# A ScalarE copy of one PSUM bank, and another buffer for one late weight, in a two-layer encoder trunk

## The chip, the cores and the metric

The kernel runs on one core of a Trainium2 chip. The metric is the device time of one execution in microseconds (us), as the median of several runs. Five engines work side by side, each through its own queue in order: PE (TensorE, matmuls), DVE (VectorE), ACT (ScalarE), POOL (GpSimd) and SP (SyncE). SP and POOL issue most of the transfers (DMA). A line number such as L1157 is a line of the kernel before; the changed kernel's lines lie 2 to 5 further down.

## The reference

One batch of 512 tokens with 1024 channels goes through two layers. Each layer has an input projection, four attention and convolution branches, a gated merge and an output projection, and then a feed-forward block:

```python
def _conv_ffn(h, w_up, conv_w, conv_b, w_down):
    u = _depthwise_conv(h @ w_up, conv_w, conv_b)
    gate, up = jnp.split(u, 2, axis=-1)
    return (jax.nn.silu(gate) * up) @ w_down

x = x + _conv_ffn(_rmsnorm(x, g_ffn[l]), w_up[l], ffn_conv_w[l], ffn_conv_b[l], w_down[l])
```

`w_up` is 1024 x 5632 (2816 gate and 2816 up channels), the depthwise convolution has width 3, all in float32. The change lies in `h @ w_up` of both layers.

## The kernel before

**Weights.** Every weight arrives as a tile of 128 x 1024 (`raw`, by a DMA of SP). ACT rounds it to `w_hi` (1.06 us), DVE subtracts to get `w_lo` (1.22 us), and PE sums three products, high by high, high by low and low by high. `w_hi` and `w_lo` have three buffers each, and weights are made two ahead of their use. `weights` (L239 and on) does this for plain weights, `seven_unit` (L1308 and on) for those below. The tiles of a plain weight come in turn from two buffers, tag `w_raw`; in the down projection, which comes next, two of four tiles come from two more, tag `w_more`.

**The up-projection.** It is cut into 11 groups of 2 x 256 output channels (two blocks of 128 gate channels and two of up channels). Groups 0, 1, 9 and 10 go as plain blocks. Groups 2 to 8 go as a product of 2 x 2 blocks with seven multiplications in place of eight: the units A11, S3, A22, S2, A12, S1, S4. A unit is 24 matmuls of 256 columns, a plain block 24 of 512. Three of the units' weights are loaded. The other four are sums of quarters and are made in the loaded tile: POOL adds a further quarter to it by an accumulating DMA (L1306) once the step before has made its `w_lo`. So A11, S3, S2 and S4 share one tile, called `chain` (tag `w_more`, two buffers, held from A11 to S4), and A22 and S1 share another (tag `w_raw`). When S4 of a group has made its `w_lo`, the chain buffer is free, and SP loads A11 of two groups on.

The groups are interleaved. Around group g, PE runs S2(g), A12(g), S1(g), S3(g+1), S4(g), A22(g+1), A11(g+2), then S2(g+1) and so on. At the end, where no further group follows, two plain blocks of group 9 are put among the last units, the `held` steps: ... A22(8), block 18.0, S2(8), A12(8), S1(8), block 18.1, S4(8). Their results stay in PSUM until they are taken out after S4(8).

**The banks.** A11, S2, S1 and S4 of a group add up in one PSUM bank (`aux`), and what it holds is taken out after each of them before the next may write. After A11, S3 and S2 it is ACT that copies the bank to an SBUF tile `sv` (L1145), ahead of other work (`with self.first()` raises the priority). After S1, DVE subtracts the bank from `sv` directly (L1157), also with raised priority. Then U0 is written (L1158), and `conv_part(…, 0)` computes the convolution of the gate blocks for both blocks of the group: an activation into cy0 on ACT (L1174), two updates on DVE (L1175, L1176), a silu on ACT (L1180). After S4 come U1 (L1162), cy1 in the same way, and the product f (L1191).

**The order.** The program's text gives the instructions, and a scheduler with priorities arranges each engine's queue when the kernel is built. Weight loading has raised priority over 3000 places. Within an engine the queue then runs in that order, each instruction waiting for its inputs and buffers.

Of the kernel before, what the change touches and what calls it, by code (L numbers as in the profile page):

```python
# [14 lines left out]
F32 = mybir.dt.float32  # L15
F32R = mybir.dt.float32r
I32 = mybir.dt.int32
AF = mybir.ActivationFunctionType
ALU = mybir.AluOpType
# [3 lines left out]
P = 128  # L23
L = 2
D = 1024
S = 512
KT = D // P
NB = S // P
DFF = 2816
# [9 lines left out]
def up_steps():  # L39

    whole = lambda g: [('whole', 2 * g + i, s) for i in range(2) for s in range(2)]
    slots = {}
    for i, g in enumerate(SEVEN):
        for n, at in (('A11', 0), ('S3', 4), ('A22', 6), ('S2', 8), ('A12', 9), ('S1', 10), ('S4', 12)):
            slots[7 * i + at] = ('seven', g, n)
    steps = [w for g in range(SEVEN[0]) for w in whole(g)]
    after = [w for g in range(SEVEN[-1] + 1, NP2) for w in whole(g)]
    own = [slots[t] for t in sorted(slots)]
    late = [('held',) + w[1:] for w in after[:2]]
    own = own[:-4] + late[:1] + own[-4:-1] + late[1:] + own[-1:]  # L50
    return steps[:-2] + own[:1] + steps[-2:] + own[1:] + [('free',) + w[1:] for w in after[:2]] + after[2:]


UP_STEPS = up_steps()

GATE_STEPS = [('ga', 'A11'), ('ga', 'A12'), ('gb', 'A11'), ('gb', 'A12'), ('ga', 'S3'), ('gb', 'S3'), ('ga', 'A22'),
              ('gb', 'A22'), ('ga', 'S2'), ('gb', 'S2'), ('ga', 'S1'), ('gb', 'S1'), ('ga', 'S4'), ('gb', 'S4')]
# [173 lines left out]
class Trunk:  # L231
# [7 lines left out]
    def weights(self, upto, ahead=3000, parts=1, queue=None):  # L239

        nc = self.nc
        while self.w_emitted < min(upto, len(self.w_list)):
            n, pieces = self.w_list[self.w_emitted]
            if n == 'seven':
                with self.tc.high_priority(offset=ahead):
                    self.w_ready.append(self.seven_unit(*pieces))
                self.w_emitted += 1
                continue
            with self.tc.high_priority(offset=ahead):

                self.w_fast = (self.w_fast + 1) % 4 if n == 0 else 0
                if n == 0 and self.w_fast in (3, 0):
                    raw = self.fp.tile([P, 1024], F32, name="w_raw", tag="w_more", bufs=2)
                else:
                    raw = self.wpool.tile([P, 1024], F32, name="w_raw", tag="w_raw", bufs=2)
                hi = self.wpool.tile([P, 1024], F32R, name="w_hi", tag="w_hi", bufs=3)
                lo = self.wpool.tile([P, 1024], F32R, name="w_lo", tag="w_lo", bufs=3)
                src = pieces()
                n = sum(p.shape[1] for p in src)
                if len(src) == 1:  # L260
                    cut = [slice(i * n // parts, (i + 1) * n // parts) for i in range(parts)]
                    src = [src[0][:, s] for s in cut]
                c = 0
                for p in src:
                    (queue or nc.sync).dma_start(raw[:, c:c + p.shape[1]], p)
                    c += p.shape[1]
                for i in range(parts):
                    s = slice(i * n // parts, (i + 1) * n // parts)
                    w = nc.scalar.activation(hi[:, s], raw[:, s], AF.Copy)  # L269
                    self.first_hi = self.first_hi or w  # L270
                    nc.vector.tensor_tensor(lo[:, s], raw[:, s], hi[:, s].bitcast(F32), ALU.subtract)  # L271
            self.w_ready.append((hi, lo))
            self.w_emitted += 1
# [842 lines left out]
    def seven(self, g, n):  # L1116

        nc = self.nc
        v = nc.vector
        st = self.sevens.setdefault(g, {})  # L1120
        bank = {'S3': 'B', 'A22': 'B', 'A12': 'C'}.get(n, 'A')
        start = n in ('S3', 'A11', 'A12')
        if start:
            st[bank] = self.mm() if bank == 'C' else self.aux()
        ps = st[bank]
        hi, lo = self.unit()
        for e in range(2):
            o = ps[:, e * 256:(e + 1) * 256]
            for j in range(4):
                s = slice((2 * j + e) * P, (2 * j + e + 1) * P)  # L1130
                xh, xl = self.seven_x(n, j)
                for i, (w, x) in enumerate(((hi, xh), (hi, xl), (lo, xh))):
                    self.last_mm = nc.tensor.matmul(o, lhsT=w[:, s], rhs=x, start=start and not (e or j or i),  # L1133
                                                    stop=j == 3 and i == 2, skip_group_check=True)
            if e == 0:
                self.tick()
        self.tick()
        two = lambda t: t.rearrange("p (e q) -> p e q", e=2)
        half = lambda h: self.RB[:, h * 256:(h + 1) * 256].unsqueeze(1).broadcast_to([P, 2, 256])
        place = lambda r, h: self.U[1 - r][:, :, 1 + h * 256:257 + h * 256]  # L1140
        tags = {'A11': 0, 'S3': 2, 'S2': 4}
        if n in tags:
            st[n] = self.fp.tile([P, S], F32, name="sv", tag=f"e{tags[n] + g % 2}", bufs=1)
            with self.first():
                nc.scalar.activation(st[n], ps, AF.Copy)  # L1145
        if n == 'S2':
            t = st['S2']
            v.tensor_tensor(t, st['B'], t, ALU.subtract)
            v.tensor_tensor(place(1, 0), two(t), half(0), ALU.mult)
        elif n == 'A12':  # L1150
            t = st['A11']
            v.tensor_tensor(t, t, ps, ALU.add)
            v.tensor_tensor(place(0, 0), two(t), half(0), ALU.mult)
        elif n == 'S1':
            t = st['S3']
            with self.first():
                v.tensor_tensor(t, t, ps, ALU.subtract)  # L1157
            v.tensor_tensor(place(1, 1), two(t), half(1), ALU.mult)  # L1158
            for i in range(2):
                self.conv_part(2 * g + i, 0)  # L1160
        elif n == 'S4':
            v.tensor_tensor(place(0, 1), two(ps), half(1), ALU.mult)  # L1162
            for i in range(2):
                self.conv_part(2 * g + i, 1)
# [70 lines left out]
    def ffn(self, l, last):  # L1235
# [12 lines left out]
        self.pace = 0.0  # L1248
        for kind, a, b in UP_STEPS:
            if kind == 'seven':  # L1250
# [267 lines left out]
    def run(self):  # L1518
        nc, tc = self.nc, self.tc
        with ExitStack() as st:  # L1520
# [10 lines left out]
            for l in range(L):  # L1531
                off, quads, quarters, ups, mixing = 0, [], {}, {}, []
                for kind, a, n in UNITS:
                    src = self.W[l, off:off + n * P].rearrange("(p c) -> p c", p=P)
                    off += n * P
                    if kind == 'quad':
                        quads.append(src)
                    elif kind == 'quarter':
                        quarters[a] = src
                    elif kind == 'up':  # L1540
                        ups[a] = src
                    elif kind == 'mixing':
                        mixing.append(src)
                    else:
                        if kind == 'out' and a == 0:
                            for i, (g, s) in enumerate(GATE_STEPS):
                                self.w_list.append(('seven', (l, g, s)))
                                if i >= 12:
                                    self.w_list.append((n, lambda m=mixing[i > 12]: [m]))
                        self.w_list.append((n, lambda src=src: [src]))  # L1550
                for kind, a, b in UP_STEPS:
                    if kind == 'seven':
                        self.w_list.append((kind, (l, a, b)))
                    elif kind != 'free':
                        self.w_list.append((1024, lambda src=ups[b * DFF + a * P]: [src]))
                self.quarters.append(quarters)
                self.quads.append(quads)
                self.sums.append([])
                self.all_quads.append(self.W[l, off - NP2 * 2048 * P:off].rearrange("(p c) -> p c", c=2048))
                self.last_units(l)  # L1560
# [10 lines left out]
            with tc.tile_pool(name="first", bufs=1, reuse_waits="tile") as first:  # L1571
# [4 lines left out]
                ps = self.aux()  # L1576
# [162 lines left out]
```

## Time and profile before

| | |
|---|---|
| median of the runs | 1534.66 us (1534.36 to 1537.81, 3 runs) |
| profiled execution | 1535.51 us, of which the profile's span is 1533.7 us |
| granted TensorE clock | 1.0 of full speed |
| up-projection, groups 2 to 8, layer 0 | about 463 to 627 us of the span |
| the same, layer 1 | about 1226 to 1391 us |
| ACT, making `w_hi` (L269, L1324) | 242.2, 75.9 and 56.9 us in its three groups |
| DVE, making `w_lo` (L271, L1325) | 280.5, 87.7 and 65.8 us in its three groups |
| load of a `w_raw` tile by SP, issue to landing | 4.4 us median |
| load or growth of a `chain` tile by POOL | 5.8 us median |

A row of the time view gives the start within the span, the duration, the engine, the line, the operation and its tiles; in brackets stands how long the engine sat idle before it and what ended that. A row of waits gives who waited for whom, the total, how often, and the longest. In a group of instructions, "x14 | 9.5, 680" means 14 instructions, 9.5 us busy together, 680 ns each on average. PE's matmuls are pipelined, so that each starts before the end drawn for the one ahead. Idle time of an engine matters only where PE, or what ends last, waits for it.

### The profile page before, as it was taken

What the parts mean: (1) busy time and instruction counts of PE and PEld (TensorE: products, weight loads), DVE (VectorE), ACT (ScalarE), POOL (GpSimd) and SP (SyncE); (2) the same over time, 40 slices, a digit from 0 to 9 for tenths busy, and PEclk for the clock granted to TensorE, in tenths of its full rate; (3) what the DMA queues carried; (4) which work ended last, traced back from release to release, by engine and by line L of the source; (5) the groups of instructions that cost most, each with busy time, mean ns of one, the idle gap of its engine ahead of it and who ended that gap; (6) DMA issues with size and microseconds to landing.
All of it is one profiled execution on the core that took longest, in us unless ns stands there. A gap on an engine that the chain in (4) does not pass through costs nothing.

```text
span 1533.7 us, 23233 instructions
## 1 busy us (share of the span) xinstructions
PE 1525.5 (99%) x8418; PEld 1326.0 (86%) x8418; DVE 1303.2 (85%) x2198; ACT 958.4 (62%) x1592; POOL 207.2 (14%) x312
## 2 busy tenths in 40 slices
PE   9999999999999999999999999999999999999999
PEld 8888888889889999888888888888898899998887
DVE  6689988888789998998576899887986899989984
ACT  6677777456456665675557687673564555656743
POOL 0123002221001111000001130022200011110100
PEclk9999999999999999999999999999999999999999
DMA  7779585857656888486568796867566589975785
GB/s 236 222 230 208 154 182 158 178 160 164 207 165 152 181 178 180 135 251 213 180 184 256 202 199 174 181 158 174 151 164 219 165 181 227 196 168 148 206 261 160
DMA packets 119490, 288.04 MB, mean 188 GB/s; under 512 B 27728, under 2 KB 29648, under 8 KB 119376
## 3 DMA queue, kind: packets, MB, share of 16 engines
q1 hardware_dynamic: 86224, 185.88, 38.0%
q0 software_dynamic: 32864, 100.15, 34.2%
q8 instruction: 66, 1.08, 0.3%
q10 hardware_dynamic: 288, 0.52, 0.1%
q14 instruction: 48, 0.39, 0.1%
HBM read 262.40 MB, written 58.72 MB: 209 GB/s over the span
## 4 chain that ended last, share of the span: by engine, by line
PE 81%; DVE 10%; ACT 3%; DMA 3%; issue 2%; SPq 0%; ACTq 0%; DVEq 0%
PE mm L291 12%; PE mm L290 12%; PE mm L292 12%; PE aux L1133 9%; PE aux L936 5%; PE aux L1416 3%; PE aux L1417 3%; PE aux L1415 3%; PE mm L520 2%; PE mm L522 2%; PE mm L521 2%; DMA chain<-W 2%; PE mm L1415 2%; PE mm L1416 2%; PE mm L1417 2%
## 5 line engine op out<-in xcount | busy, mean ns | idle before, releaser
L269 ACT ACTIVATE w_hi<-w_raw 128x1024 fp32r<-128x1024 f32 (+1 forms) x233 | 242.2, 1040 | 211.1 <-PE mm L291 83.7
L271 DVE TENSOR_TENSOR w_lo<-w_raw,w_hi 128x1024 fp32r<-128x1024 f32 (+1 forms) x233 | 280.5, 1206 | 63.8 <-ACT w_hi L269 62.7
L290 PE MATMUL mm<-xh,w_hi 128*128 128x512 f32 x704 | 275.3, 391 | 0.0
L291 PE MATMUL mm<-xl,w_hi 128*128 128x512 f32 x704 | 274.7, 390 | 0.0
L292 PE MATMUL mm<-xh,w_lo 128*128 128x512 f32 x704 | 274.4, 390 | 0.0
L1133 PE MATMUL aux<-form,w_hi 128*128 128x256 f32 x896 | 163.7, 284 | 1.5 <-ACT sv L1145 1.4
L292 PEld LDWEIGHTS mm<-xh,w_lo 128*128 128x128 f32 x704 | 132.2, 188 | 28.0
L290 PEld LDWEIGHTS mm<-xh,w_hi 128*128 128x128 f32 x704 | 132.2, 188 | 26.5
L291 PEld LDWEIGHTS mm<-xl,w_hi 128*128 128x128 f32 x704 | 132.3, 188 | 26.0
L1133 PEld LDWEIGHTS aux<-form,w_hi 128*128 128x128 f32 x896 | 139.9, 192 | 2.8 <-ACT sv L1145 2.5
L1133 PE MATMUL aux<-form,w_lo 128*128 128x256 f32 x448 | 126.9, 283 | 0.0
L1324 ACT ACTIVATE w_hi<-chain 128x1024 fp32r<-128x1024 f32 x72 | 75.9, 1056 | 56.4 <-DMA chain<-W 17.8
L1325 DVE TENSOR_TENSOR w_lo<-chain,w_hi 128x1024 fp32r<-128x1024 f32 x72 | 87.7, 1220 | 16.7 <-ACT w_hi L1324 15.4
L457 DVE SCALAR_TENSOR_TENSOR cv<-cv,prm 128x512 f32<-128x512 f32 x120 | 94.5, 788 | 0.7
L1324 ACT ACTIVATE w_hi<-w_raw 128x1024 fp32r<-128x1024 f32 x54 | 56.9, 1055 | 50.1 <-PE aux L1133 19.4
L1133 PEld LDWEIGHTS aux<-form,w_lo 128*128 128x128 f32 x448 | 86.0, 192 | 0.2 <-DVE w_lo L1325 0.2
L1306 POOL DMA_DIRECT2D chain<-W x54 | 47.3, 875 | 272.8 <-DVE w_lo L1325 251.7
L1174 ACT ACTIVATE cy<-U,prm 128x512 f32<-128x512 f32 x88 | 68.0, 808 | 21.1 <-DVE U L1158 13.8
L520 PE MATMUL mm<-w_hi,xh 128*128 128x512 f32 x192 | 76.4, 398 | 0.3 <-DVE V L648 0.3
L521 PE MATMUL mm<-w_lo,xh 128*128 128x512 f32 x192 | 75.0, 390 | 0.0
L522 PE MATMUL mm<-w_hi,xl 128*128 128x512 f32 x192 | 74.8, 391 | 0.0
L1325 DVE TENSOR_TENSOR w_lo<-w_raw,w_hi 128x1024 fp32r<-128x1024 f32 x54 | 65.8, 1218 | 9.6 <-ACT w_hi L1324 8.9
(379 smaller groups left out, 3921.8 us busy)
## 6 DMA issues: line engine op xcount, KB each, us to landing
w_raw<-W SPq DMA_DIRECT2D x187, 512.0 KB, 4.4
chain<-W POOLq DMA_DIRECT2D x54, 512.0 KB, 5.8
sums<-W POOLq DMA_DIRECT2D x24, 1024.0 KB, 11.9
w_raw<-W SPq DMA_DIRECT2D x66, 256.0 KB, 4.0
w_raw<-sums SPq DMA_DIRECT2D x44, 256.0 KB, 4.1
w_raw<-sums SPq DMA_DIRECT2D x22, 512.0 KB, 4.6
sums<-W POOLq DMA_DIRECT2D x12, 768.0 KB, 9.7
chain<-W SPq DMA_DIRECT2D x18, 512.0 KB, 5.2
```

The costliest lines, as they stand in the source:

```text
L269: w = nc.scalar.activation(hi[:, s], raw[:, s], AF.Copy)
L271: nc.vector.tensor_tensor(lo[:, s], raw[:, s], hi[:, s].bitcast(F32), ALU.subtract)
L290: mm(ps, lhsT=wh, rhs=xh, start=start, stop=False)
L291: mm(ps, lhsT=wh, rhs=xl, start=False, stop=False)
L292: self.last_mm = mm(ps, lhsT=wl, rhs=xh, start=False, stop=stop)
L457: self.after_mm(v.scalar_tensor_tensor(acc, u[:, t:t + S], w(t), acc, ALU.mult, ALU.add))
L520: mm(pss[b], lhsT=self.Xh[k][:, t], rhs=hi[:, s], start=k == 0, stop=False)
L521: mm(pss[b], lhsT=self.Xh[k][:, t], rhs=lo[:, s], start=False, stop=False)
L522: self.last_mm = mm(pss[b], lhsT=self.Xl[k][:, t], rhs=hi[:, s], start=False, stop=k == KT - 1)
L1133: self.last_mm = nc.tensor.matmul(o, lhsT=w[:, s], rhs=x, start=start and not (e or j or i), stop=j == 3 and i == 2, skip_group_check=True)
L1324: nc.scalar.activation(hi, raw, AF.Copy)
L1325: nc.vector.tensor_tensor(lo, raw, hi.bitcast(F32), ALU.subtract)
```

## The change

There are two edits. After S1, ACT copies the bank to an SBUF tile (the two tags e6 and e7, one buffer each, by the group's parity) with raised priority, and DVE subtracts that copy, at ordinary priority. And the last held block's weight (18.1 in each layer) is loaded into a tile of the tag `w_more`, which the chains use, and not `w_raw`; it is marked by the number 3 in place of 1024 in the list of weights, a number that is used for nothing else there.

```diff
+LATE = [w for w in UP_STEPS if w[0] == 'held'][-1]
...
-                if n == 0 and self.w_fast in (3, 0):
+                if n == 0 and self.w_fast in (3, 0) or n == 3:
                     raw = self.fp.tile([P, 1024], F32, name="w_raw", tag="w_more", bufs=2)
                 else:
                     raw = self.wpool.tile([P, 1024], F32, name="w_raw", tag="w_raw", bufs=2)
...
         elif n == 'S1':
             t = st['S3']
+            a = self.fp.tile([P, S], F32, name="sv", tag=f"e{6 + g % 2}", bufs=1)
             with self.first():
-                v.tensor_tensor(t, t, ps, ALU.subtract)
+                nc.scalar.activation(a, ps, AF.Copy)
+            v.tensor_tensor(t, t, a, ALU.subtract)
             v.tensor_tensor(place(1, 1), two(t), half(1), ALU.mult)
             for i in range(2):
                 self.conv_part(2 * g + i, 0)
...
-                        self.w_list.append((1024, lambda src=ups[b * DFF + a * P]: [src]))
+                        n = 3 if (kind, a, b) == LATE else 1024
+                        self.w_list.append((n, lambda src=ups[b * DFF + a * P]: [src]))
```

The scheduler orders the queues anew. DVE's queue around S1 of group 5 in layer 0, before (the first row is the subtract; the `w_lo` of chain_6162 is that of the A11 two groups on, the one of chain_5917 is S2 of the group after):

```order
L1157 TENSOR_TENSOR sv_5872<-sv_5872,aux_5703 128x512
L1158 TENSOR_TENSOR U0_4726<-sv_5872,RB_4788 128x2x256
L1325 TENSOR_TENSOR w_lo_6122<-w_raw_6119,w_hi_6121 128x1024
L1175 SCALAR_TENSOR_TENSOR cy0_6076<-U0_4726,prm_73,cy0_6076 128x512
L1175 SCALAR_TENSOR_TENSOR cy0_6082<-U0_4726,prm_73,cy0_6082 128x512
L1176 SCALAR_TENSOR_TENSOR cy0_6076<-U0_4726,prm_73,cy0_6076 128x512
L1325 TENSOR_TENSOR w_lo_6165<-chain_6162,w_hi_6164 128x1024
L1176 SCALAR_TENSOR_TENSOR cy0_6082<-U0_4726,prm_73,cy0_6082 128x512
L1162 TENSOR_TENSOR U1_4729<-aux_5703,RB_4788 128x2x256
L1325 TENSOR_TENSOR w_lo_6195<-chain_5917,w_hi_6194 128x1024
```

The same place after the change (chain_6170 is the A11, chain_5923 the S2):

```order
L1329 TENSOR_TENSOR w_lo_6130<-w_raw_6127,w_hi_6129 128x1024
L1161 TENSOR_TENSOR sv_5878<-sv_5878,sv_6080 128x512
L1162 TENSOR_TENSOR U0_4726<-sv_5878,RB_4788 128x2x256
L1329 TENSOR_TENSOR w_lo_6173<-chain_6170,w_hi_6172 128x1024
L1179 SCALAR_TENSOR_TENSOR cy0_6084<-U0_4726,prm_73,cy0_6084 128x512
L1179 SCALAR_TENSOR_TENSOR cy0_6090<-U0_4726,prm_73,cy0_6090 128x512
L1329 TENSOR_TENSOR w_lo_6203<-chain_5923,w_hi_6202 128x1024
L1180 SCALAR_TENSOR_TENSOR cy0_6084<-U0_4726,prm_73,cy0_6084 128x512
L1180 SCALAR_TENSOR_TENSOR cy0_6090<-U0_4726,prm_73,cy0_6090 128x512
L1166 TENSOR_TENSOR U1_4729<-aux_5707,RB_4788 128x2x256
```

The subtract has moved behind one `w_lo`, and the cy0 updates, three of which stood ahead of the A11's `w_lo`, all stand behind it.

SP's queue at the end of the up-projection of layer 0, before (w_raw_6652 is block 18.0, w_raw_7293 a tile of the down projection, w_raw_6712 A12 of group 8, w_raw_6777 block 18.1):

```order
L265 DMA w_raw_6652<-W 128x1024
L265 DMA w_raw_7293<-W 128x512
L265 DMA w_raw_7293<-sums0_680 128x512
L1318 DMA w_raw_6712<-W 128x1024
L265 DMA w_raw_6777<-W 128x1024
L265 DMA w_raw_6850<-W 128x1024
```

And after (block 18.0 is w_raw_6664, block 18.1 w_raw_6789, A12 w_raw_6724, the down projection's tile w_raw_7307):

```order
L267 DMA w_raw_6664<-W 128x1024
L267 DMA w_raw_6789<-W 128x1024
L1322 DMA w_raw_6724<-W 128x1024
L267 DMA w_raw_6864<-W 128x1024
L267 DMA w_raw_6939<-W 128x1024
L267 DMA w_raw_7307<-W 128x512
L267 DMA w_raw_7307<-sums0_680 128x512
```

The load of 18.1 now stands ahead of A12's, and the down projection's tile behind two later plain blocks.

ACT's queue around the same S1 of group 5, before (chain_6162 is the A11):

```order
L1324 ACTIVATE w_hi_6121<-w_raw_6119 128x1024
L1174 ACTIVATE cy0_6076<-U0_4726,prm_73 128x512
L1174 ACTIVATE cy0_6082<-U0_4726,prm_73 128x512
L1145 ACTIVATE sv_6117<-aux_6088 128x512
L1324 ACTIVATE w_hi_6164<-chain_6162 128x1024
L1180 ACTIVATE fth_6080<-cy0_6076 128x512
```

In the changed kernel (sv_6080 is the new copy, sv_6125 that of S3's bank, chain_6170 the A11):

```order
L1328 ACTIVATE w_hi_6129<-w_raw_6127 128x1024
L1160 ACTIVATE sv_6080<-aux_5707 128x512
L1147 ACTIVATE sv_6125<-aux_6096 128x512
L1328 ACTIVATE w_hi_6172<-chain_6170 128x1024
L1178 ACTIVATE cy0_6084<-U0_4726,prm_73 128x512
L1178 ACTIVATE cy0_6090<-U0_4726,prm_73 128x512
```

The new copy stands where the cy0 activations stood, and these have moved behind the copy of S3's bank and behind the `w_hi` of the A11.

## The prediction

> **What bounds the kernel now.** I read the page first, then the views of waits, windows and time around the up-projection, where all of the change lies.
>
> ```profile
> span 1533.7 us, 23233 instructions
> PE 1525.5 (99%) x8418; PEld 1326.0 (86%) x8418; DVE 1303.2 (85%) x2198; ACT 958.4 (62%) x1592; POOL 207.2 (14%) x312
> PE aux L1133 <- ACT sv L1145: 1.4, 2, 0.8
> PE aux L1133 <- DVE sv L1157: 0.4, 2, 0.2
> ```
>
> PE, the engine of the matmuls, is busy 99% of the span; the last two rows are all that PE waits for on the two edited paths (total us, times, longest). So this change can win little. PE's end of a matmul is modelled: the seven products' matmuls start every 0.12 us but are drawn 0.28 long, so each stall is some 0.16 longer than its row says.
>
> The two waits for L1145 are the copy of the bank behind S2 of group 8, once in each layer:
>
> ```profile
> 594.63 1.22 DVE L1325 TENSOR_TENSOR w_lo<-chain,w_hi 128x1024 fp32r<-128x1024 f32 x1
> 608.25 1.23 DVE L1325 TENSOR_TENSOR w_lo<-w_raw,w_hi 128x1024 fp32r<-128x1024 f32 x1 [1.17 <-ACT w_hi L1324]
> 609.50 7.46 SPq L265 DMA_DIRECT2D w_raw<-W  x3
> 612.29 0.28 PE L1133 MATMUL mm<-xh,w_hi 128*128 128x256 f32 x1
> 614.29 1.06 ACT L269 ACTIVATE w_hi<-w_raw 128x1024 fp32r<-128x1024 f32 x1 [3.80 <-DMA w_raw<-W]
> 615.26 0.58 ACT L1145 ACTIVATE sv<-aux 128x512 f32<-128x512 f32 x1
> 615.89 0.50 PE L1133 MATMUL aux<-form,w_hi 128*128 128x256 f32 x2 [0.56 <-ACT sv L1145]
> 1378.71 1.06 ACT L269 ACTIVATE w_hi<-w_raw 128x1024 fp32r<-128x1024 f32 x1 [2.00 <-DMA w_raw<-W]
> 1379.67 0.58 ACT L1145 ACTIVATE sv<-aux 128x512 f32<-128x512 f32 x1
> ```
>
> The load of 18.1, the second late plain block, starts at 609.50, when w_lo of g8's A12 (608.25 + 1.23) has freed its buffer. ACT sits idle 3.80 us for it and then makes its w_hi; the copy that S1 on PE needs stands behind that in ACT's queue. S2's matmuls end when A12's begin (612.29), but S1's begin only at 615.89, 3.60 us later, where a unit takes 2.88. (594.63 is w_lo of g7's S4, used below.)
>
> **The rhythm that the change touches** is DVE's. Each group's period on PE is seven units of 24 matmuls at 0.12 us, 2.88 us each, 20.16 in all. Beside it runs a loop: w_lo of S4 frees a chain buffer, SP loads A11 of two groups on into it, ACT makes w_hi, DVE makes w_lo of A11 and works through its queue to w_lo of the next S4.
>
> ```profile
> 499.44 1.23 DVE L1325 TENSOR_TENSOR w_lo<-chain,w_hi 128x1024 fp32r<-128x1024 f32 x1 [0.19 <-ACT w_hi L1324]
> 513.14 1.22 DVE L1325 TENSOR_TENSOR w_lo<-chain,w_hi 128x1024 fp32r<-128x1024 f32 x1
> 519.05 1.06 ACT L1324 ACTIVATE w_hi<-chain 128x1024 fp32r<-128x1024 f32 x1 [0.70 <-DMA chain<-W]
> 520.14 1.23 DVE L1325 TENSOR_TENSOR w_lo<-chain,w_hi 128x1024 fp32r<-128x1024 f32 x1 [0.73 <-ACT w_hi L1324]
> 533.30 1.22 DVE L1325 TENSOR_TENSOR w_lo<-chain,w_hi 128x1024 fp32r<-128x1024 f32 x1
> 540.75 1.23 DVE L1325 TENSOR_TENSOR w_lo<-chain,w_hi 128x1024 fp32r<-128x1024 f32 x1 [1.18 <-PE aux L1133]
> 553.47 1.22 DVE L1325 TENSOR_TENSOR w_lo<-chain,w_hi 128x1024 fp32r<-128x1024 f32 x1
> 560.50 1.06 ACT L1324 ACTIVATE w_hi<-chain 128x1024 fp32r<-128x1024 f32 x1 [1.84 <-DMA chain<-W]
> 561.59 1.23 DVE L1325 TENSOR_TENSOR w_lo<-chain,w_hi 128x1024 fp32r<-128x1024 f32 x1 [1.86 <-ACT w_hi L1324]
> 563.75 0.28 PE L1133 MATMUL aux<-xl,w_hi 128*128 128x256 f32 x1
> 563.87 0.28 PE L1133 MATMUL aux<-xh,w_lo 128*128 128x256 f32 x1
> 574.32 1.22 DVE L1325 TENSOR_TENSOR w_lo<-chain,w_hi 128x1024 fp32r<-128x1024 f32 x1
> 581.91 1.22 DVE L1325 TENSOR_TENSOR w_lo<-chain,w_hi 128x1024 fp32r<-128x1024 f32 x1 [1.32 <-ACT w_hi L1324]
> 584.03 0.28 PE L1133 MATMUL aux<-xh,w_lo 128*128 128x256 f32 x1
> ```
>
> These are layer 0's rows in order of time: A11 (499.44, 520.14, 540.75, 561.59, 581.91), S4 between them, and PE's first matmuls with w_lo of A11 (g7 563.87, g8 584.03). A11's loops take 20.70, 20.61, 20.84 and 20.32 us, longer than PE's 20.16: the slack falls from group to group, to 563.87 − 562.82 = 1.05 and 584.03 − 583.13 = 0.90. Layer 0 ends just before it would stall.
>
> How long DVE needs from w_lo of A11 to the end of w_lo of S4 depends on what stands between. With one cy0 update between them it is 13.95 us (561.59 to 574.32 + 1.22). Layer 1 shows the other case, all four cy0 updates between:
>
> ```profile
> 1325.17 1.23 DVE L1325 TENSOR_TENSOR w_lo<-chain,w_hi 128x1024 fp32r<-128x1024 f32 x1 [2.43 <-ACT w_hi L1324]
> 1339.15 1.21 DVE L1325 TENSOR_TENSOR w_lo<-chain,w_hi 128x1024 fp32r<-128x1024 f32 x1
> 1345.74 1.23 DVE L1325 TENSOR_TENSOR w_lo<-chain,w_hi 128x1024 fp32r<-128x1024 f32 x1 [1.84 <-ACT w_hi L1324]
> 1355.06 1.22 DVE L1325 TENSOR_TENSOR w_lo<-w_raw,w_hi 128x1024 fp32r<-128x1024 f32 x1
> 1359.72 1.22 DVE L1325 TENSOR_TENSOR w_lo<-chain,w_hi 128x1024 fp32r<-128x1024 f32 x1
> 1361.46 0.68 DVE L1157 TENSOR_TENSOR sv<-sv,aux 128x512 f32<-128x512 f32 x1
> ```
>
> That is 15.19 (1325.17 to 1340.36) and 15.20 us, with a longer idle hole ahead of A11's w_lo (2.43 and 1.84 us). Here S4 on PE waited for L1157 in two groups (the second at 1361.46).
>
> **The change part by part.** The sum is made against the profiled execution, 1535.51 us with a span of 1533.7; it is 0.85 above the median of the runs, 1534.66, to which I add the difference in the end. Runs of before lie between 1534.36 and 1537.81, and about 0.3%, 4.6 us, is what a measurement can tell from no change.
>
> *The operations.*
>
> ```profile
> L1191 DVE TENSOR_TENSOR f<-cy,fth 128x512 f32<-128x512 f32 x44 | 29.6, 682 | 0.1
> L1145 ACT ACTIVATE sv<-aux 128x512 f32<-128x512 f32 x42 | 24.4, 581 | 4.8 <-PE aux L1133 4.8
> L1157 DVE TENSOR_TENSOR sv<-sv,aux 128x512 f32<-128x512 f32 x14 | 9.5, 680 | 0.0
> ```
>
> The new copy is L1145's kind, 0.58 us, 14 times 8.1 us on ACT, which is idle 38% of the span. DVE saves nothing: a subtract with both inputs in SBUF costs as much (L1191, 682 ns) as the one that reads PSUM (L1157, 680). What changes is who frees bank A for S4. [...]
>
> *S4 released by ACT.* The two waits of 0.2 us, each 0.36 with the modelled end, go: up to 0.7 us in layer 1. Layer 0 has no such wait.
>
> *18.1's load is moved.* Its tile now comes from the two chain buffers, free at w_lo of g7's S4 (594.63 + 1.22), 13.6 us earlier, and SP issues it ahead of A12's load. Then w_hi of 18.1 waits only for a w_hi buffer, which S2 on PE frees at 612.3; w_hi and the copy end 1.06 + 0.58 later, near 614.0, ahead of 615.2, where S1 would start unheld. The stalls go: 0.8 us in layer 0 (0.6 by the waits view and 0.16) and 1.0 in layer 1. SP now issues A12's load behind one more; that one's buffer is free sooner, so it blocks nothing, and the down-projection load that left its place was as large.
>
> *The reordering that comes with it.* With the subtract one engine hop later and at ordinary priority, the four cy0 updates of a group stand behind w_lo of A11's chain in all of layer 0's groups. They no longer fill the hole; DVE waits there with them queued behind, and must do them inside the section: 15.2 us in place of 13.95. Who waits is S4's w_lo, so the next load, so the next A11. From 499.44 on, with each load and w_hi as long as its rows give (from S4's w_lo end to A11's w_lo: 5.78, 6.23, 6.90, 6.37): 499.44 + 15.2 + 5.78 = 520.42, then 541.85, 563.95, 585.52. A11 slips by 0.28, 1.10, 2.36 and 3.61 us; slack covers 1.05 and 0.90, so PE is late by 1.31 at g7's A11 and by 2.71 in all at g8's. Behind it w_lo of S1 ends 10.54 us after A11's begins (1345.74 to 1356.28), and PE needs it 1.23 + 3 × 2.88 = 9.87 after: 0.7 more, 3.4 together. If every load were as quick as the one before 519.05 (4.69 us after 514.36), A11 would slip by 1.45 at g8, past the slack by 0.55, with S1 1.2. The ends are 0 (a hole that fills otherwise) and 3.4; I take 3.0, near the end that the loads' own rows give.
>
> *Layer 1* had this order already in its last groups. By my count of the new queue, one earlier section grows by about 1.5 us and a neighbour shrinks by 1.2, transposes having moved into the hole: 0, between −0.7 and +2.2. Its end is DVE's:
>
> ```profile
> 1365.65 0.33 SPq L1318 DMA_DIRECT2D w_raw<-W  x1
> 1373.86 1.23 DVE L1325 TENSOR_TENSOR w_lo<-w_raw,w_hi 128x1024 fp32r<-128x1024 f32 x1 [3.85 <-ACT w_hi L1324]
> 1386.00:1406.00 20.00, 20.00 (x101) 17.03 (x100) 20.00 (x30) 13.55 (x18) 0.90 (x1) 1.00 0.54 153
> 1426.00:1436.00 10.00, 9.87 (x44) 7.85 (x43) 9.03 (x16) 10.00 (x14) 1.74 (x2) 1.00 0.97 230
> ```
>
> In a windows row the columns behind the length are PE, PEld, DVE, ACT, POOL. DVE is full from 1386 to 1406, and PE already loses 0.13 us behind 1426. DVE's run begins with A12's w_lo at 1373.86, whose load starts when 18.0's w_lo is done and which the change leaves there. What PE gains at S4 and S1 it waits for later: layer 1 gives 0.
>
> *Sum:* −0.8 + 3.0 in layer 0, 0 in layer 1: +2.2 us. 1535.51 becomes 1537.7, and the median 1534.66 becomes **1536.9**, 0.14% longer: no change that can be told.
>
> **The rivals.**
> *The gain stands* (the waits go, the loop doesn't bind). For it: layer 0 has no stall at A11 now, and loads vary (4.69 to 5.81 us from w_lo to w_hi). Against it: the falling slack. It gives −0.8 in layer 0 and −0.7 to −1.7 in layer 1: 1532.2 to 1533.2.
> *The loop binds in both layers*, so it ends slower: layer 0 pays 3.4 − 0.8 = 2.6, and in layer 1 the longer section delays A11 of g7 by up to 2.2, with it 18.0's w_lo, A12's load and so the whole DVE-bound tail: +4.8, 1539.5; with S1's 0.7 a second time 1540.2. It decides once layer 1's loads leave the neighbour no chance to win its 1.2 back; the hole of 2.43 us already there speaks for it, the idle DVE in that hole against.
> *The change doesn't do what it says*: 18.1's w_hi keeps its place ahead of the S2 copy in ACT's queue, and if its load still came late (the DMA queue, the chain buffer), the 0.8 would stay: +3.0, 1537.7. Against it: the buffer is free 13.6 us before.
>
> **How the numbers follow.** Forecast 0.55, gain stands 0.24, binds in both 0.13, load still late 0.08. The range goes from 1532.4 to 1540.6. Faster by over 0.3% needs 1530.0, more than all waits on the edited paths: 0.03. Slower by over 0.3% needs 1539.3, the second rival and a little of the first case's tail: 0.13. The rest, 0.84, is within.
>
> **What would show it.** In the profile of after: no PE wait for the S2 copy at g8; S4 no longer waiting for DVE; ACT's w_hi of 18.1 at about 612.4. If the loop binds, the idle time ahead of w_lo<-chain grows towards 2 to 3 us in layer 0, w_lo of S4 ends 15.2 us after A11's begins, and PE waits for w_lo at A11 of g7 and g8 and at S1. In layer 1 DVE stays full behind 1374, with PE's wait behind 1426 grown. I am wrong if A11's sections stay near 14 us or its loads shorten as they move.

## The result, and the profile after

| | before | after |
|---|---|---|
| median of the runs | 1534.66 us (1533.39 to 1537.81, 7 runs) | 1543.97 us (1539.49 to 1547.90, 7 runs) |
| profiled execution | 1535.51 us, span 1533.7 | 1542.23 us, span 1540.5 |
| granted TensorE clock, profiled execution | 1.0 | 1.0 |
| granted TensorE clock, single runs of after | | 0.997 to 1.0 |

The changed kernel is slower: ratio 1.0060, 95% interval 1.0043 to 1.0078. The forecast was 1536.9 us, and the range ended at 1540.6.

First the page of after, its span and its row of busy times:

```profile
span 1540.5 us, 23241 instructions
PE 1526.4 (99%) x8418; PEld 1326.9 (86%) x8418; DVE 1302.9 (85%) x2198; ACT 964.3 (63%) x1606; POOL 206.9 (13%) x312
```

PE's and DVE's work is what it was; ACT has its 14 copies more. So the 6.8 us of span are waits. PE's waits in after (for whom, total us, times, longest):

```profile
PE aux L1420 <- DVE w_lo L273: 5.2, 2, 2.7
PE aux L1135 <- DVE w_lo L1329: 1.5, 3, 0.8
...
PE mm L1419 <- DVE U L1267: 0.4, 1, 0.4
PE aux L755 <- DMA KL<-KL: 0.4, 1, 0.4
```

Both waits that the change was to touch are gone: there is no row for the copy behind S2 and none for the subtract or its copy ahead of S4. But the first row, 5.2 us in two waits, had no counterpart in before, and L1420 is no line of the up-projection. It is a matmul of the down projection, in the steps that begin it while the up-projection's last results are still taken out. Here is the place in layer 0, in after's order of time (start, us, engine, line, tiles, idle time ahead and what ended it), from ACT, POOL, DVE and PE:

```profile
664.44 1.04 ACT L271 ACTIVATE w_hi<-w_raw 128x1024 fp32r<-128x1024 f32 x1
665.38 1.05 ACT L1217 ACTIVATE plo<-pfh 128x1024 fp32r<-128x1024 f32 x1
666.72 0.87 POOL L1218 DMA_DIRECT2D plo<-f  x1 [6.54 <-ACT pe L1224]
670.78 0.41 DVE L1402 TENSOR_TENSOR sum<-sum,f 128x256 f32<-128x256 f32 x1
674.38 0.39 PE L1419 MATMUL aux<-w_hi,pfh 128*128 128x512 f32 x1
675.57 0.69 DVE L1398 TENSOR_TENSOR pfp<-f,pxl 128x512 fp32r<-128x512 f32 x1 [4.38 <-DMA plo<-f]
676.18 1.22 DVE L273 TENSOR_TENSOR w_lo<-w_raw,w_hi 128x1024 fp32r<-128x1024 f32 x1
677.46 0.50 PE L1420 MATMUL aux<-w_lo,pfh 128*128 128x512 f32 x1 [2.68 <-DVE w_lo L273]
```

Read it from the bottom. PE waits for a `w_lo`. That one's inputs are long there, but in DVE's queue it stands behind `pfp<-f,pxl` (L1398), the first subtract for the seventh pair of the product's inputs. This one writes a buffer that an accumulating transfer of POOL for the fifth pair (`plo<-f`, L1218) is still reading, and DVE sits idle 4.38 us until the transfer is through. The transfer is issued once ACT has made `plo` (L1217), and ACT makes a `w_hi` ahead of that. (The POOL row names `pe`, which ACT was making in the same moment; from the end of `plo` to the issue it is 0.3 us, as in before.)

The same place in before:

```profile
663.37 1.04 ACT L1213 ACTIVATE plo<-pfh 128x1024 fp32r<-128x1024 f32 x1
664.32 1.04 ACT L269 ACTIVATE w_hi<-w_raw 128x1024 fp32r<-128x1024 f32 x1
664.71 0.87 POOL L1214 DMA_DIRECT2D plo<-f  x1 [5.59 <-ACT plo L1213]
672.04 0.69 DVE L1394 TENSOR_TENSOR pfp<-f,pxl 128x512 fp32r<-128x512 f32 x1 [1.66 <-DMA plo<-f]
672.65 1.22 DVE L271 TENSOR_TENSOR w_lo<-w_raw,w_hi 128x1024 fp32r<-128x1024 f32 x1
673.60 0.39 PE L1415 MATMUL aux<-w_hi,pfh 128*128 128x512 f32 x1
673.92 0.50 PE L1416 MATMUL aux<-w_lo,pfh 128*128 128x512 f32 x1
```

The trap was there already: DVE sat idle 1.66 us for the same transfer, and `w_lo` ended (672.65 + 1.22 = 673.87) just as PE came to it. In after ACT's two rows have changed places, which makes `plo` 0.94 us later (665.38 − 664.44). The whole section is 1.07 us later besides (664.44 − 663.37), and the transfer takes 675.57 − 666.72 = 8.85 us from issue to its reader, where it took 672.04 − 664.71 = 7.33. Together `w_lo` ends 677.40 − 673.87 = 3.53 us later. PE comes only 674.38 − 673.60 = 0.78 later, so 2.8 us are a stall: 0.94 from the exchanged rows, 1.5 from the longer transfer and 0.3 from the section, which is later than PE by that much. In layer 1 it is 2.6 by the same reading of these two rows of after:

```profile
1442.59 0.39 PE L1419 MATMUL aux<-w_hi,pfh 128*128 128x512 f32 x1
1445.46 0.50 PE L1420 MATMUL aux<-w_lo,pfh 128*128 128x512 f32 x1 [2.48 <-DVE w_lo L273]
```

### The profile page after: what moved, and what is told of

Its sections match the earlier page's. It is cut to its first block, busy times and chain, and to the rows that moved or that the text cites. A ratio compares the mean times of both kernels' runs of the same rounds, so it can differ in the third digit from the quotient of the medians.

```text
span 1540.5 us, 23241 instructions
## 1 busy us (share of the span) xinstructions
PE 1526.4 (99%) x8418; PEld 1326.9 (86%) x8418; DVE 1302.9 (85%) x2198; ACT 964.3 (63%) x1606; POOL 206.9 (13%) x312
## 4 chain that ended last, share of the span: by engine, by line
PE 74%; DVE 14%; DMA 4%; ACT 4%; issue 3%; SPq 0%; DVEq 0%; ACTq 0%
PE mm L292 12%; PE mm L293 12%; PE mm L294 12%; PE aux L1135 7%; PE aux L938 4%; DVE w_lo L1329 3%; PE aux L1420 2%; PE aux L1421 2%; PE aux L1419 2%; DVE w_lo L273 2%; PE mm L522 2%; PE mm L523 2%; PE mm L524 2%; DMA chain<-W 2%; DVE cy L1180 2%
```

## The experiments

Line numbers of copies with an edit differ from after's by up to five. The first nine kernels ask who makes the new wait, and what is gained without it; the last three ask why the runs of after differ by more (9.3 us) than the two profiled executions do (6.7).

### Which of the two edits

Only the second, 18.1's weight in a chain's buffer:

```diff
             with self.first():
-                nc.scalar.activation(a, ps, AF.Copy)
-            v.tensor_tensor(t, t, a, ALU.subtract)
+                v.tensor_tensor(t, t, ps, ALU.subtract)
```

> Only the second edit: block 18.1's weight in a chain's buffer; the subtract behind S1 stays on DVE from PSUM. Tail theory (the loss of the changed kernel lies in the down projection's start, where w_lo stands in DVE's queue behind a subtract that waits for an early pair's POOL transfer, and that queue order comes with the ScalarE copy): no PE wait over 0.3 us for w_lo there, the two stalls for the S2 copy at group 8 gone, 0 to 1.9 us faster than before (ratio 0.9988 to 1.000). Loop theory (the loss lies in the reordered loops of the up-projection): the same, since those queues stay as before. If the late weight itself were to blame, this kernel would be 3 us or more slower than before.

1534.32 us against 1534.72, ratio 0.9996 (0.9987 to 1.0005). Its waits:

```profile
PE aux L1135 <- DVE w_lo L1327: 0.8, 2, 0.5
...
PE aux L1418 <- DVE w_lo L273: 0.3, 1, 0.3
```

No copy behind S2 is waited for and the down projection starts nearly without a stall. But nothing is gained that can be measured.

Only the first, the copy:

```diff
-                if n == 0 and self.w_fast in (3, 0) or n == 3:
+                if n == 0 and self.w_fast in (3, 0):
...
-                        n = 3 if (kind, a, b) == LATE else 1024
-                        self.w_list.append((n, lambda src=ups[b * DFF + a * P]: [src]))
+                        self.w_list.append((1024, lambda src=ups[b * DFF + a * P]: [src]))
```

> Only the first edit: the ScalarE copy behind S1; 18.1's weight as before. Tail theory: the tail's queues are those of the changed kernel, so PE waits 2 to 3 us for w_lo at the start of the down projection in each layer, and the S2-copy stalls of group 8 (0.8 and 1.1 us) are there as well: 5 to 8 us slower than before. Loop theory: slower by what the loops lose, 1 to 3 us, and no wait of 2 us in the tail. If the late weight is to blame: as before.

1543.31 us, ratio 1.0058 (1.0045 to 1.0071): the whole loss.

```profile
PE aux L1418 <- DVE w_lo L271: 5.0, 2, 2.8
PE aux L1133 <- DVE w_lo L1327: 2.2, 3, 0.8
...
PE aux L1133 <- ACT sv L1145: 0.2, 1, 0.2
```

The 5.0 us belong to the copy: ACT's and DVE's queues are after's, row for row and buffer numbers aside, while those of the second edit alone are before's. The last row is a miss: with 18.1's load where it was, I expected the stalls of 0.8 and 1.1 us at the S2 copy to stay, and 0.2 was left of them. The time is a miss too, 8.9 us over before by the ratio where I expected 5 to 8; all five runs have a clock below 1.0, which the last experiments look into.

### Is the subtract of the seventh pair the cause?

After, with the pairs' splitting begun two steps later, and the seventh pair's first subtract held until a matmul of that step:

```diff
-            v.tensor_tensor(l, x, h.bitcast(F32), ALU.subtract)
+            w = v.tensor_tensor(l, x, h.bitcast(F32), ALU.subtract)
+            if l is kl and j == len(EARLY):
+                self.paced(w)
...
-            if todo:
+            if todo and j > 1:
```

> The changed kernel, with the first subtract of the seventh pair's split (the one that waits for the early pair's transfer) put behind the w_lo for which PE waits: the pairs' splits begin two steps later in the down projection and that subtract waits for a matmul. Tail theory: both waits of 2.7 us go, the time is 4.5 to 5.5 us below the changed kernel's, so within +0 to +2.5 us of before. Loop theory: the changed kernel's time, within 1 us.

1535.42 us, ratio 1.0009 (1.0001 to 1.0018), and the row is gone from the waits, though ACT's two rows stand exchanged as in after. So the loss hangs on that subtract in front of that `w_lo`. The median is 8.5 us below after's, more than the 4.5 to 5.5 expected: what after's runs lose beyond its profiled stalls goes with the stalls. What is left of both edits is 1.4 us (0.2 to 2.8) over before by the ratio. Where it lies is not shown, for the profiled execution, 1535.21 us, took no longer than before's.

After, with ACT's order mended at these two rows: `plo` ahead of the `w_hi`.

```diff
-        nc.scalar.activation(low, hi.bitcast(F32), AF.Copy, scale=-1.0)
+        with self.first():
+            nc.scalar.activation(low, hi.bitcast(F32), AF.Copy, scale=-1.0)
```

> The changed kernel, with raised priority for the ScalarE instruction that starts an early pair's low part, so that in ACT's queue it stands ahead of the down projection's w_hi again, as before the change. Tail theory: pair 4's POOL transfer is issued about 0.95 us earlier, and PE's wait in each layer falls from 2.8 to between 0.4 (if the transfer is as quick as in the kernel before) and 1.9 us: 1.9 to 4.9 us below the changed kernel. Loop theory: the changed kernel's time, within 1 us.

1541.01 us, ratio 1.0040 (1.0027 to 1.0052).

```profile
PE aux L1421 <- DVE w_lo L273: 3.3, 2, 1.8
```

The wait falls by 5.2 − 3.3 = 1.9 us, 0.95 in each layer, which looks like the 0.94 between the two places. That is luck, for the edit did not move these two rows alone. In layer 0 the transfer is 0.64 us shorter than in after besides (8.21 in place of 8.85), but DVE's queue has changed as well: two more subtracts of the split (`f<-f` and `sum<-sum,f`) now stand between `pfp` and the `w_lo` and take 0.67. So ACT's order is a part of the wait, and how large a part alone is not shown.

### Which of the fourteen copies

The copy in all groups but the last, group 8 (the diff is against after), and, with `==` in place of `<`, only in the last:

```diff
+            if g < SEVEN[-1]:
                 a = self.fp.tile([P, S], F32, name="sv", tag=f"e{6 + g % 2}", bufs=1)
                 with self.first():
                     nc.scalar.activation(a, ps, AF.Copy)
                 v.tensor_tensor(t, t, a, ALU.subtract)
+            else:
+                with self.first():
+                    v.tensor_tensor(t, t, ps, ALU.subtract)
```

> The changed kernel, but group 8 of each layer keeps the DVE subtract from PSUM; six of seven groups have the ScalarE copy. Its queues at the start of the down projection are those of before. Tail theory (one copy, the last, flips the tail's order, and that is the loss): PE's waits there fall from 2.7 us to under 0.6, the loops of the up-projection stay as in the changed kernel (about 1.2 us of waits in layer 0), and the time is within 2 us of before, 4.5 us or more below the changed kernel. Loop theory (all copies share in the loss): six sevenths of it stay, 6 us over before.

> The changed kernel, with the ScalarE copy in group 8 alone; the other six groups subtract from PSUM on DVE. Its tail has the changed kernel's queues, its loops those of before. Tail theory: PE waits 2 to 3 us for w_lo at the start of the down projection in each layer: 3.5 to 6 us slower than before. Loop theory: one seventh of the loss, within 1.5 us of before.

All but the last: 1536.68 us, ratio 1.0011 (1.0002 to 1.0020). Its waits:

```profile
PE aux L1135 <- DVE w_lo L1333: 1.5, 2, 0.8
...
PE aux L1424 <- DVE w_lo L273: 0.3, 1, 0.3
```

Only the last: 1542.09 us, ratio 1.0044 (1.0031 to 1.0057).

```profile
PE aux L1424 <- DVE w_lo L273: 4.5, 2, 2.4
```

One copy of 0.58 us in each layer makes most of the loss: 6.8 us by the ratio (4.8 to 8.7), about 4.5 of it the profiled waits; I expected 3.5 to 6. The twelve others, with 18.1's load moved, cost 1.7 us (0.3 to 3.1), near the +2.2 that the prediction summed up for both edits. With group 8's copy the scheduler builds this ACT order at the start of the down projection, where without it the two rows stand the other way round:

```
L271 ACTIVATE w_hi<-w_raw 128x1024
L1217 ACTIVATE plo<-pfh 128x1024
```

### Is it the work, or the change of dependence?

Before, with an additional ScalarE copy after each S1, of 512 columns from SBUF to SBUF, in the same buffers as the change's copy, which nothing reads:

```diff
+            a = self.fp.tile([P, S], F32, name="sv", tag=f"e{6 + g % 2}", bufs=1)
             with self.first():
                 v.tensor_tensor(t, t, ps, ALU.subtract)
+            nc.scalar.activation(a[:, :512], t[:, :512], AF.Copy)
```

> The kernel before with one more ScalarE copy per group, of the subtracted tile from SBUF to the tags e6 and e7, read by nobody; the DVE subtract from PSUM stays. The order of the other instructions stays as before. Tail theory: the copies' own 14 x 0.6 us lie in ScalarE's idle time, so the time is that of before within 1 us. If ScalarE's load were the cause, 3 us or more slower.

1534.41 us, ratio 1.0001 (0.9992 to 1.0010). Fourteen more ACT instructions cost nothing, and the tail's order stays. So neither the number of ACT's instructions nor the buffers reorder the tail. What is left of the edit is the hop (the subtract that depends on the copy) and the priorities (the copy's raised, the subtract's no longer); which of the two does it was not tried, and by which of its rules the scheduler then exchanges the two rows was not followed.

### Is there a better version?

The later splitting, by the diff above, in before and beside the second edit alone:

> The kernel before, with the first subtract of the seventh pair's split put behind the w_lo, as in e4_split_behind: the control for that run. Tail theory: before's waits at that place are 0.1 and 0.2 us only, so nothing to gain: within 0.7 us of before. If the move gained by itself, e4's recovery would not speak for the tail: 3 us or more faster than before.

> A version that might beat both: the second edit alone (18.1's weight in a chain's buffer), with the split's subtract behind the w_lo. It has the loops of before, no S2-copy stall at group 8 (0.8 and 1.1 us) and no wait at the split (0.1 and 0.4 us). Tail theory: 0 to 2 us faster than before, at the edge of what the runs can tell; layer 1's gain may be waited away in its tail. If slower by 1 us or more, the early load costs something that these runs have not shown.

1534.22 us, ratio 0.9998 (0.9988 to 1.0007), and 1533.18 us, ratio 0.9993 (0.9984 to 1.0002). Neither can be told from before. So the later splitting gives nothing by itself and only takes out after's stall.

Before with later splitting has the queues of before around S2 of group 8, and yet ACT and PE do this there:

```profile
609.18 1.06 ACT L1324 ACTIVATE w_hi<-w_raw 128x1024 fp32r<-128x1024 f32 x1 [2.72 <-PE mm L291]
612.12 1.06 ACT L269 ACTIVATE w_hi<-w_raw 128x1024 fp32r<-128x1024 f32 x1 [1.87 <-PE aux L1133]
613.08 0.58 ACT L1145 ACTIVATE sv<-aux 128x512 f32<-128x512 f32 x1
```

18.1's `w_hi` (the second row) waits for PE's S2, not for its load, and the copy stands at 613.08 where before's profiled execution had it at 615.26. The load of A12 had landed earlier, its `w_lo` ended at 607.73 (609.48 in before) and freed 18.1's buffer sooner. So the stall of 0.8 us that the second edit takes away is not in every execution; the run with the additional copies, whose queues are before's there too, shows no such wait either.

### The clock behind a stall

In the copy-alone run, the profile's windows around the stall in layer 0 (length, PE busy and matmuls, granted clock, share of DMA, GB/s):

```profile
673.00:674.00 1.00, 1.00 (x6) 1.00 1.00 322
...
675.00:676.00 1.00, 0.00 (x0) 1.00 1.13 285
...
677.00:678.00 1.00, 0.82 (x2) 0.50 1.05 240
...
679.00:680.00 1.00, 1.00 (x4) 0.50 0.91 301
...
681.00:682.00 1.00, 1.00 (x6) 1.00 0.98 348
```

Behind the stall PE runs at half its clock for some 3 us; after's profiled execution shows 1.00 until 1539.55 us, behind its last matmul (which starts at 1536.34). To see whether a stall does this anywhere, I made stalls far from the edits, in before: at every eighth plain block ACT rewrites `w_lo` in place, two or three times, behind the block ahead.

```diff
+        self.blocks = getattr(self, 'blocks', 0) + 1
+        if self.blocks % 8 == 0:
+            with self.first():
+                for _ in range(2):
+                    self.paced(self.nc.scalar.activation(lo, lo.bitcast(F32), AF.Copy))
         for k in range(KT):
             s = slice(k * P, (k + 1) * P)
```

> Before, with ten PE stalls made on purpose, at every eighth plain block far from both edits: ACT rewrites w_lo twice in place (1.06 us each), behind the last matmul of the block ahead, and PE's third product waits for it: about 2.1 - 0.5 = 1.6 to 2.2 us of stall each, 16 to 22 us in all. Theory (a stall itself makes the granted clock drop behind it, as behind the stalls of 2.84 us in the copy-alone run and of 1.83 us in the low-first run): some of the ten, at least two, are followed by about 3.4 us at a granted clock of 0.5, and the time grows by 1.6 to 1.7 us more for each; the mean clock of the span falls below 1.0. Rival (the drop belongs to the start of the down projection, or is chance): the clock stays 1.0 behind all ten, and the time grows by the stalls alone.

> The same ten places with three rewrites: stalls of about 2.7 to 3.3 us each, 27 to 33 us in all. Theory: more of the ten are followed by the drop than with two rewrites, since a longer stall is likelier to cause it; time = stalls + about 1.65 us a drop. Rival: no drop, or as many as with two, and the time differs by the stalls alone, some 11 us from the other.

> The changed kernel once more, unedited. If the clock makes up the 2.6 us by which the runs differ more than the profiled executions, most runs have a mean clock of 0.997 to 0.999, each 0.001 worth 1.5 us, and the time less (1 - clock) x span stands 5.5 to 7 us above before in all of them. If it doesn't, the spread of the times has nothing to do with their clocks.

Two rewrites: 1557.27 us, ratio 1.0157 (1.0142 to 1.0172); three: 1564.72, 1.0203 (1.0189 to 1.0216). All eight runs had a mean clock of 0.995 to 0.997, while before's 11 had 1.0. The places were eleven, not ten, and the scheduler spread the stalls to other lines too. PE around one of them, with two rewrites:

```profile
450.10 0.39 PE L290 MATMUL mm<-xh,w_hi 128*128 128x512 f32 x1
450.33 0.39 PE L291 MATMUL mm<-xl,w_hi 128*128 128x512 f32 x1
453.27 0.79 PE L292 MATMUL mm<-xh,w_lo 128*128 128x512 f32 x1 [2.55 <-ACT w_lo L315]
453.86 0.63 PE L290 MATMUL mm<-xh,w_hi 128*128 128x512 f32 x1
454.29 0.63 PE L291 MATMUL mm<-xl,w_hi 128*128 128x512 f32 x1
...
456.94 0.39 PE L292 MATMUL mm<-xh,w_lo 128*128 128x512 f32 x1
457.17 0.39 PE L290 MATMUL mm<-xh,w_hi 128*128 128x512 f32 x1
```

The starts are 0.23 us apart ahead of the stall, 0.43 behind it, and 0.23 again from 456.94. Counted over seven profiles (after twice, the copy alone, the copy in the last group, `plo` first, and the two made for this), by the idle time that PE's row shows (the wait of 1.2 us at the start of every program left out):

| idle time of PE | followed by the half clock | not |
|---|---|---|
| 2.1 us and more | 7 (2.39, 2.55, 2.83, 3.03, 3.45, 3.46, 6.97) | 6 (2.12, 2.18, 2.32, 2.48, 2.57, 2.68) |
| 1.3 to 1.9 us | 2 (1.32, 1.83) | 7 |
| 0.7 to 1.2 us | 0 | 9 |

Each drop costs 1.6 to 1.7 us (the sum of (1 − clock) over the windows behind it), 2.1 behind the longest. So a stall can lower the clock behind it, not at the start of the down projection alone, though not each time, and the rival falls. That three rewrites give more drops than two did not come true: two against three.

The traces also show which stalls do it. In them the recorded clock changes only on a grid of 3.41 us: in the copy-alone run its records begin at 4.57, 676.99, 680.41 and 1540.57 us, which lie 197, 1 and 252 steps apart, and where the grid lies differs between executions (the first record begins at 5.50 us in before's profile and at 6.97 in after's). I added up PE's idle time step by step in all fourteen profiles, the two ends of the program left out. Each of the ten steps with 1.83 us or more of it was followed by a step at half clock, and none of the others was, the largest with 1.74. So in these profiles it is the idle time within one step that tells the two apart, and not the length of a stall. After's stall of 2.68 us fell into two steps, with 1.21 and 1.48, and the clock stayed 1.0; the stall of 1.32 had another 0.57 in its step, 1.89 together, and the clock fell.

After once more: 1542.73 us (1537.35 to 1549.45, 6 runs), ratio 1.0062 (1.0044 to 1.0079), five of the six runs below 1.0. Here my expectation was only half right. Less (1 − clock) x span the six runs lie from 2 to 10 us above before, not all between 5.5 and 7: the clock is a part of the spread only. The mean moreover takes in the end of the span: in after's profiled execution the clock is at 0.5 from 1539.55 us to the end at 1540.46, 0.0003 of the mean. How much of a 0.999 comes from there in the single runs was not shown. What else spreads the runs of after over 12 us stays open; the length of the transfer, and so of the stall, is one candidate, for without the stall (after with the later splitting) the runs lie within 4 us.

## Why the prediction was wrong

**What bounds the kernel, and the small gain: right.** PE was the bound and stayed at 99%; the edits' own waits were the 1.8 us of the two quoted rows.

**S2's copy, −0.8: the mechanism right, the term one execution's.** In after ACT's `w_hi` of 18.1 starts at 614.14, just when S2 has freed its buffer, where I forecast 612.4 for a schedule that was then 1.7 us earlier, and PE doesn't wait. But the stall is all but absent without the edit as well, in the copy-alone run (0.2), in before with the later splitting and in before with the additional copies, and the second edit alone changed nothing that can be measured. I had one profile and took its load time for the kernel's.

**S4 released by ACT: right.** No S4 waits for DVE in after.

**The loop in layer 0, +3.0: the mechanism right, the size double.** The rows of `w_lo<-chain` in after, A11 and S4 by turns:

```profile
499.63 1.23 DVE L1329 TENSOR_TENSOR w_lo<-chain,w_hi 128x1024 fp32r<-128x1024 f32 x1 [1.11 <-ACT w_hi L1328]
...
513.77 1.22 DVE L1329 TENSOR_TENSOR w_lo<-chain,w_hi 128x1024 fp32r<-128x1024 f32 x1
...
521.06 1.23 DVE L1329 TENSOR_TENSOR w_lo<-chain,w_hi 128x1024 fp32r<-128x1024 f32 x1 [2.38 <-ACT w_hi L1328]
...
555.51 1.22 DVE L1329 TENSOR_TENSOR w_lo<-chain,w_hi 128x1024 fp32r<-128x1024 f32 x1
...
561.91 1.23 DVE L1329 TENSOR_TENSOR w_lo<-chain,w_hi 128x1024 fp32r<-128x1024 f32 x1 [1.52 <-ACT w_hi L1328]
...
575.89 1.22 DVE L1329 TENSOR_TENSOR w_lo<-chain,w_hi 128x1024 fp32r<-128x1024 f32 x1
...
583.72 1.23 DVE L1329 TENSOR_TENSOR w_lo<-chain,w_hi 128x1024 fp32r<-128x1024 f32 x1 [2.94 <-ACT w_hi L1328]
```

The section is 575.89 + 1.22 − 561.91 = 15.20 us, as forecast, and the idle time ahead grows to 2.94. What I held fixed was the way from S4's `w_lo` to the next A11's: I put 6.90 for the one that ends at 561.9, and it took 561.91 − 556.73 = 5.18. So the slip at g7 stayed within the slack, and PE lost 0.8 us at g8's A11 and 0.7 behind it, 1.5 in place of 3.0, by the starts of its matmuls against before's (of the 1.5 in the row of waits above only 0.5 is this place). The run with the copy in all groups but the last puts the up-projection's cost over both layers, gains taken off, at the 1.7 us above.

**Layer 1, 0: wrong, and with it what I left out of layer 0.** This is the step that failed: "The reordering that comes with it" was followed only as far as the cy0 updates and A11's `w_lo` in the up-projection. The words "What PE gains at S4 and S1 it waits for later: layer 1 gives 0" named the end as DVE's but took its queue, and ACT's, to stand as before. The start of the down projection was costed at nothing in both layers, and the copy of group 8 reorders it: 5.5 us of stalls in after by the starts of PE's rows (2.8 and 2.6), against 0.3 in before. Layer 1's up-projection itself came out near the 0, at −0.4, but by luck: PE lost 1.6 us at one A11 and some 0.4 at a later `w_lo`, while two S4 and the S2 copy gave 1.8 back, and smaller places 0.6. Beside the 5.2 of new stalls the profiled difference of 6.7 holds 1.5 − 0.8 = 0.7 in layer 0's up-projection, this −0.4, 0.7 in the attention (most at one transfer, the row of L755), which the change doesn't touch, 0.3 at the start of the program, and the rest in smaller waits.

**The step from the profile to the median: wrong in size.** I added the difference in the end, as if both kernels' executions were alike. Before's profiled execution was 0.85 above its median, after's 1.74 below. Both profiled executions showed a clock of 1.0, while most runs of after don't; and one drop is some 1.65 us. 6.7 + 0.85 + 1.74 is the 9.3 of the medians.

**The rivals.** None of the three held the mechanism. The one that came out on the slower side, the loop in both layers at 1539.5 to 1540.2, had the sign and not the place: the loops of both layers cost 1.4 to 1.7 us more by the two kernels without the stall. DVE gains nothing by the copy: by the rows of after its subtract took 683 ns each, in place of 680 before:

```profile
L1161 DVE TENSOR_TENSOR sv<-sv 128x512 f32<-128x512 f32 x14 | 9.6, 683 | 0.0
L1160 ACT ACTIVATE sv<-aux 128x512 f32<-128x512 f32 x14 | 8.1, 579 | 0.0
```

## What to carry to other kernels

Where a scheduler orders the queues, compare them from the edit to the end of the program, the stage after the edited one too: look there for an instruction that waits for a transfer and has a weight's `w_lo` behind it in an in-order queue, and ask how little margin it has (here 1.66 us of idle DVE with PE just served). A stall in one profile may be that execution's; see it in a second one before an edit is made against it. And price a PE stall above its length: in these profiles, where 1.83 us or more of idle time fell into one step of 3.41 us, it cost 1.6 to 1.7 us more, and 2.1 behind the longest.

## What the runs showed of the hardware that was not expected

- A PE stall of 1.32 us and longer was followed by about 3.4 us at half clock in 9 of 22 cases, in stages far apart. The recorded clock changed on a grid of 3.41 us that lay elsewhere in each of three executions (first records at 4.57, 5.50 and 6.97 us). All ten steps with 1.83 us or more of idle time were followed by the drop, and none with 1.74 or less: a stall of 1.83 us was, and one of 2.68, cut by the grid into 1.21 and 1.48, was not.
- The accumulating transfer of the fifth pair took 5.8 to 8.0 us from issue to landing in the twelve cases with the tail's order of before (before, the second edit alone, the copy in all groups but the last, the additional copies, the two with the later splitting without the copy) and 8.3 to 9.3 in the ten with the order of after (after twice, the copy alone, the copy in the last group, after with the later splitting); with `plo` first it was 8.2 and 7.8. After with the later splitting has no stall, so the length goes with the order and not with the stall. Why it is longer with that order was not shown.
- Fourteen further ScalarE copies of 512 columns made no difference (ratio 1.0001), while one copy in each layer that a subtract depends on made 1.0044 (with 18.1's load moved, which alone made 0.9996).
